# Delta rule of a hybrid decoder: score products in banks of their own, samples' states in two halves from POOL's queue, prompt's state products four steps later

## The chip, the cores and the metric

The kernel runs on one core of one Trainium2 chip, as one program. The metric is the device time of one execution in microseconds (us). Engines are named as in the profile: PE multiplies matrices (PEld loads its stationary operand), DVE, ACT and POOL work on vectors, SP only issues transfers.

## What is computed (the reference, cut)

Two consecutive decoder layers, for a prompt of 256 positions and for 8 samples of 4 positions each (32 rows), which share all weights. Layer 0 mixes tokens by retention, layer 1 by a gated delta rule; each mixer is followed by a gated feed-forward network with a short causal convolution. The change lies in layer 1's mixer alone:

```python
proj = einsum('btd,de->bte', h, w_in)                # q, k, v, gate z, and b, a
conv = silu(causal_dwconv(q|k|v, conv_buf, w_conv))
q, k = l2norm(q) * 128**-0.5, l2norm(k)              # 8 key heads, 16 value heads of 128
beta = sigmoid(b);  g = -exp(a_log) * softplus(a + dt_bias)
def step(S, chunk):                                   # 64 positions of the prompt
    G = cumsum(g);  decay = exp(G_i - G_j), lower triangle
    L = strict_lower((k*beta) @ k.T * decay)          # the scores of the solve
    u, w = solve(I + L, [v*beta, k*beta*exp(G)])
    v_new = u - w @ S
    o = (q*exp(G)) @ S + ((q @ k.T) * decay) @ v_new  # the scores of the attention
    S = S * exp(G_last) + (k*exp(G_last - G)).T @ v_new
out = (rmsnorm(o) * silu(z)) @ w_out
```

For the samples the same rule starts from a stored state S of 128x128 for each of 8 samples and 16 heads, and the 4 new positions form one chunk. The new states of prompt and samples are outputs too.

## The kernel before

**Products.** Every projection is `product` (L525 to L537): the weight tile is split into a rounded part `whi` (ACT, L414) and a rest `wlo` (DVE, L415), the activations likewise, and three passes of 128x288 matmuls are summed; with 1024 inputs that is 24 matmuls to one output tile of 128 columns. The 288 columns are 256 prompt positions and 32 sample rows.

**Order.** Instructions stand on each engine in the order in which a list scheduler puts the program's operations. The program itself is written with generators: after every 6 matmuls of `product` (`QUANTUM`) comes a *tick* (L482), and in each tick all side generators go one `yield` further. `pause(n)` lets n ticks go by, so n times 6 products. A matmul of `product` is called a product below, and positions are told by the number of products counted from the program's start of the mixer's stage.

**The delta-rule stage** works on 4 groups g of 2 key heads and 4 value heads. Its main line is `GDN_ORDER` (L33): K0 V0 K1 A0 Z0 V1 K2 Z1 V2 K3 D0 V3 Z2 D1 D2 Z3 D3, where K are a group's q and k projections, V its values, Z its gate, D its part of the down projection, A a piece of the conditioning vector. K, V, Z and D are 96 products each. Beside it run side generators, for each group: `gdn_decays` (products `pd`, then ACT copies and an exponential into `gat`; POOL's `decay` tiles at L1232 feed them), `gdn_scores`, `gdn_inverse` and levels `pe` (the solve), `gdn_samples` (the samples), `gdn_finish` (the prompt's output and new state).

**Scores** (L1261 to L1284). For each of two key heads j, PE writes `pa` (128x512, L1275) and `pb` (128x256, L1276) from `kqT`; DVE then reads both in eight instructions, L1278 to L1283, into `gnn` (scores of the solve) and `gat` (scores of the attention). DVE's first instruction needs POOL's `ksc` (L1181, L1182), which needs the norms from `pq` (PE L1168) by way of a dozen short DVE instructions. PSUM tiles come from `aux(name, tag)`: tags `a`, `c`, `e` and `s` have one bank of 2 KB per partition each, `b` and `mm` two. Both `pa` have tag `s`, both `pb` tag `a`, each a tile of its own, so j=1 is written when j=0 has been read.

**The samples' states** (L1425 to L1496). A group's states are 2 MB, read as four tiles `gS` of 512 KB (two samples each), from two buffers, by DMAs on SP's queue (L1436). `pks` (L1466) takes 128 matmuls of 128x32 by 128x128, in four runs of 32, one run to a tile; a `gS` tile is loaded again when the run that read its buffer has been issued. The results go through `t` (DVE L1473, ACT L1475) to `psy` (L1480), `t` (DVE L1482), again `psy`, and `pso` (L1489). SP's queue also carries all weights (L400) and the small rearrangements of the solve.

**The prompt's state** (`gdn_finish`). DVE scales the outputs into `on` (L1618, tile name `bigc`); after `pause(STATE_STEPS)`, one tick, PE forms the state `gpS` in 8 matmuls (L1623), whose operands are `kn` and a `bigc` that POOL wrote at L1602.

Of the kernel before, what the change touches and what calls it, by code (L numbers as in the profile page):

```python
# [6 lines left out]
F32 = mybir.dt.float32  # L7
# [7 lines left out]
P = 128  # L15
DM = 1024
KT = DM // P
TP, NB, TD = 256, 8, 4
# [14 lines left out]
GDN_ORDER = [(s[0], int(s[1])) for s in "K0 V0 K1 A0 Z0 V1 K2 Z1 V2 K3 D0 V3 Z2 D1 D2 Z3 D3".split()]  # L33
N_ADA = sum(c == "A" for c, _ in GDN_ORDER)
PAIR_STEPS = (2,2,2,1)
STATE_STEPS = 1
CONV_STEPS = 3
RAW_RET = 3
S_BUFS = 4
# [15 lines left out]
GROUP = 2  # L55
RAW = 4
BIG_C = 4
PA_TAGS = ("sa","sa")
LEVEL_STEPS = 3
LEVEL_TAG = "e"  # L60
GATE_STEPS = 3
SOLVE_STEPS = 1
SAMPLE_STEPS = 3
OUT_STEPS = 1
SQ_ADD = 5
QK_STEPS = 5
# [227 lines left out]
class Program:  # L294
# [660 lines left out]
    def gdn(self, hs, after):  # L955
        nc = self.nc
        with ExitStack() as ctx:
# [17 lines left out]
            nc.gpsimd.memset(self.TA, 0.0)  # L975
            self.gtail = t("gtail", [P, 32, 3])
            self.nexg = None
            self.spawn(self.gdn_gates(hs))
            w = self.weights("wba")
            self.pba = self.mmt("pba")  # L980
# [281 lines left out]
    def gdn_scores(self, g, d):  # L1262

        nc, gp = self.nc, self.gp
        kqT, sc, D = d["kqT"], d["sc"], d["decays"]
        nn = gp.tile([P, 4, 384], F32, tag="gnn", name=f"gnn_{g}", bufs=2)
        at = D[:, 0:12, :].rearrange("p (v b) c -> p v (b c)", b=3)
        for jt, c in ((0, TP - 1), (1, 383)):
            nc.gpsimd.tensor_copy(sc[:, 2, jt, :], at[:, :, c])
        yield  # L1270
        for j in range(2):
            if j:
                yield from self.pause(SCORE_STEPS)
            pa, pa2 = (self.aux(f"p{c}{g}{j}", t) for c, t in zip("ab", PA_TAGS[j]))
            nc.tensor.matmul(pa, lhsT=kqT[:, j, 0, 0:P], rhs=kqT[:, j, :, 0:TP], start=True, stop=True)  # L1275
            nc.tensor.matmul(pa2[:, 0:TP], lhsT=kqT[:, j, 0, P:TP], rhs=kqT[:, j, :, P:TP], start=True, stop=True)  # L1276
            for v in (2 * j, 2 * j + 1):
                nc.vector.scalar_tensor_tensor(nn[:, v, 0:P], pa[:, 0:P], sc[:, 0, 0, v : v + 1], at[:, v, 0:P], ALU.mult, ALU.mult)  # L1278
                nc.vector.scalar_tensor_tensor(nn[:, v, P:TP], pa[:, P:TP], -1.0, at[:, v, P:TP], ALU.mult, ALU.mult)
                nc.vector.scalar_tensor_tensor(nn[:, v, TP:], pa2[:, 0:P], sc[:, 0, 1, v : v + 1], at[:, v, TP:], ALU.mult, ALU.mult)  # L1280
            vs = slice(2 * j, 2 * j + 2)
            nc.vector.tensor_tensor(at[:, vs, 0:TP], pa[:, TP:].unsqueeze(1).to_broadcast([P, 2, TP]), at[:, vs, 0:TP], ALU.mult)
            nc.vector.tensor_tensor(at[:, vs, TP:], pa2[:, P:TP].unsqueeze(1).to_broadcast([P, 2, P]), at[:, vs, TP:], ALU.mult)  # L1283
        d.update(at=at, nn=nn)  # L1284
# [133 lines left out]
    def gdn_gate(self, g, hs, d):  # L1418
# [3 lines left out]
            self.nc.scalar.activation(sz[:, m, :], p, AF.Silu)  # L1422
        d["sz"] = sz

    def gdn_samples(self, g, a):  # L1425

        nc, gp, A = self.nc, self.gp, self.A
# [1 line left out]
        big = lambda sh, dt=F32: self.big(sh, dt, "s", 512, 3, 1)  # L1429
        small = lambda: gp.tile([P, P], F32, tag="t05", name=f"t05_{g}", bufs=8)  # L1430
        kqd, rr, vs = a["kqd"], a["rr"], a["vs"]
        S = []

        def load(u):
            S.append(t("gS", [P, 2, 4, P], bufs=2))
            nc.sync.dma_start(S[-1], A["sg"][g][:, 2 * u : 2 * u + 2])  # L1436

        load(0)
        load(1)

        sc = t("ssc", [P, 3], bufs=1)
        nc.vector.tensor_scalar(sc[:, 0:1], self.bs[:, g : g + 1], rr[:, 8:9], rr[:, 8:9], ALU.mult, ALU.mult)
# [14 lines left out]
        nc.vector.scalar_tensor_tensor(db, pas[:, 0:P], sc[:, 1:2], db, ALU.mult, ALU.mult)  # L1457
        nc.vector.tensor_tensor(du, pas[:, P : 2 * P], du, ALU.mult)
        pks = self.aux(f"pks{g}", "c")
        for bb in range(NB):  # L1460
            if bb % 2 == 0:
                yield

            for s in range(2):
                for v in range(4):
                    nc.tensor.matmul(  # L1466
                        pks[32 * v : 32 * v + 32, s * P : (s + 1) * P], lhsT=kqm[s][:, v // 2, bb, :], rhs=S[bb // 2][:, bb % 2, v, :],
                        start=(bb == 0 and s == 0), stop=(bb == NB - 1 and s == 1), skip_group_check=True,
                    )
            if bb % 2 and bb < 4:  # L1470
                load(bb // 2 + 2)
        r = small()
        nc.vector.scalar_tensor_tensor(r, pks[:, 0:P], self.nexg[:, g : g + 1], vs, ALU.mult, ALU.add)  # L1473
        qg = small()
# [255 lines left out]
```

## Time and profile before

| what | us |
|---|---|
| median of 3 runs | 1231.98 |
| the three runs | 1230.52 to 1234.35 |
| the profiled execution, its own time | 1235.09 |
| span of its trace, first to last instruction | 1233.3 |
| PE busy in the span | 1162.4 (94%) |
| DVE busy | 877.2 (71%) |
| ACT, POOL busy | 608.4 (49%), 326.0 (26%) |
| stage of the delta rule | about 592 to 990 |

PE is the busiest engine, so a stretch in which PE is not busy is where time is lost. DVE is next, and within the delta-rule stage its share is higher than over the whole span. The clock in the table by stretches is the granted clock of PE as a share of full speed.

### The profile page before, as it was taken

How to read it: one execution, taken by the hardware profiler on the slowest of the kernel's cores; microseconds unless marked ns; L12 is line 12 of the kernel's file. 1: busy time of each engine (PE TensorE's matmuls, PEld its weight loads, DVE VectorE, ACT ScalarE, POOL GpSimd, SP SyncE). 2: the span in 40 equal slices, each digit the busy share in tenths (PEclk: the TensorE clock that was granted, in tenths of full speed). 3: DMA queues.
4: the chain of work that ended last, by engine and by line, in shares of the span. 5: the costliest groups of instructions: out<-in, count | busy, mean ns of one | idle time of the engine just before them, and what ended most of it. 6: DMA issues, size and time to landing. Idle time of an engine off the chain costs nothing.

```text
span 1233.3 us, 24974 instructions
## 1 busy us (share of the span) xinstructions
PE 1162.4 (94%) x9486; PEld 1045.2 (85%) x9486; DVE 877.2 (71%) x2038; ACT 608.4 (49%) x1258; POOL 326.0 (26%) x504
## 2 busy tenths in 40 slices
PE   6999999999999999999889888988899899999996
PEld 2879788797969999997777777977789699999996
DVE  3657574765766666667769888797965687878785
ACT  2444534344446445543674655745544365555542
POOL 0214142151301221233242124243222212233241
PEclk9999999999999999999989998999999899999997
DMA  9999696866689556556636652534334997878521
GB/s 350 347 335 331 224 338 230 315 239 236 226 298 400 196 161 199 171 181 243 219 84 209 218 165 61 161 129 120 126 109 130 307 358 257 258 238 264 182 76 39
DMA packets 97480, 269.08 MB, mean 218 GB/s; under 512 B 26816, under 2 KB 28832, under 8 KB 97232
## 3 DMA queue, kind: packets, MB, share of 16 engines
q1 hardware_dynamic: 87456, 234.42, 56.6%
q0 software_dynamic: 8032, 29.16, 6.3%
q10 hardware_dynamic: 1872, 3.90, 0.9%
q8 instruction: 75, 1.23, 0.4%
q14 instruction: 45, 0.37, 0.1%
HBM read 236.06 MB, written 31.39 MB: 217 GB/s over the span
## 4 chain that ended last, share of the span: by engine, by line
PE 77%; DVE 13%; ACT 3%; DMA 3%; issue 2%; POOL 1%; ACTq 0%; POOLq 0%; DVEq 0%
PE down L533 17%; PE fg L533 12%; PE fv L533 11%; PE pg L533 4%; PE pv L533 4%; PE adaP L453 4%; PE p L533 3%; PE gv L533 2%; PE gz L533 2%; DVE mp L1319 2%; DVE wlo L415 2%; PE gk L533 2%; PE pO L884 1%; PE pU L903 1%; PE pS L854 1%
## 5 line engine op out<-in xcount | busy, mean ns | idle before, releaser
L415 DVE TENSOR_TENSOR wlo<-more,whi 128x1024 fp32r<-128x1024 f32 x138 | 171.1, 1241 | 80.6 <-ACT whi L414 67.8
L414 ACT CAST whi<-more 128x1024 fp32r<-128x1024 f32 x138 | 144.4, 1048 | 139.6 <-PE down L533 53.3
L414 ACT CAST whi<-raw 128x1024 fp32r<-128x1024 f32 x123 | 128.0, 1044 | 146.3 <-PE down L533 44.1
L415 DVE TENSOR_TENSOR wlo<-raw,whi 128x1024 fp32r<-128x1024 f32 x123 | 154.2, 1256 | 60.6 <-ACT whi L414 36.5
L702 POOL TENSOR_TENSOR x<-x,dt 128x32 f32<-128x32 f32 x159 | 103.1, 649 | 138.9 <-DVE dt L700 137.2
L698 DVE SCALAR_TENSOR_TENSOR x<-down,mod,x 128x256 f32<-128x256 f32 x160 | 76.7, 479 | 52.5 <-PE down L533 51.9
L580 POOL TENSOR_TENSOR fal<-cv,fah 128x288 fp32r<-128x288 f32 x44 | 41.2, 936 | 217.3 <-ACT fah L579 186.3
L533 PE MATMUL down<-fal,whi 128*128 128x288 f32 x352 | 64.5, 295 | 0.0
L533 PE MATMUL down<-fah,whi 128*128 128x288 f32 x352 | 62.2, 294 | 0.0
L533 PE MATMUL down<-fah,wlo 128*128 128x288 f32 x352 | 62.1, 294 | 0.0
L904 DVE SCALAR_TENSOR_TENSOR S<-S,pU 128x512 f32<-128x512 f32 x64 | 42.2, 684 | 24.5 <-PE pU L903 24.4
L533 PE MATMUL fg<-hh_ffn,whi 128*128 128x288 f32 x352 | 58.4, 298 | 0.8 <-ACT hh_ffn L626 0.7
L533 PE MATMUL fv<-hh_ffn,whi 128*128 128x288 f32 x352 | 58.7, 297 | 0.0
L533 PE MATMUL fg<-hh_ffn,wlo 128*128 128x288 f32 x352 | 55.0, 296 | 0.0
L533 PE MATMUL fv<-hh_ffn,wlo 128*128 128x288 f32 x352 | 54.7, 295 | 0.0
L533 PE MATMUL fv<-hl_ffn,whi 128*128 128x288 f32 x352 | 54.2, 295 | 0.0
L533 PEld LDWEIGHTS fg<-hh_ffn,whi 128*128 128x128 f32 x352 | 50.3, 188 | 4.6 <-ACT hh_ffn L632 2.2
L533 PE MATMUL fg<-hl_ffn,whi 128*128 128x288 f32 x352 | 54.0, 295 | 0.0
L533 PEld LDWEIGHTS down<-fal,whi 128*128 128x128 f32 x352 | 52.4, 188 | 0.4 <-issue 0.4
L533 PEld LDWEIGHTS down<-fah,whi 128*128 128x128 f32 x352 | 51.9, 188 | 0.8 <-ACT whi L414 0.8
L533 PEld LDWEIGHTS fv<-hh_ffn,whi 128*128 128x128 f32 x352 | 50.3, 188 | 2.5 <-ACT ftail L934 1.2
L533 PEld LDWEIGHTS down<-fah,wlo 128*128 128x128 f32 x352 | 51.9, 188 | 0.0
(467 smaller groups left out, 2921.3 us busy)
## 6 DMA issues: line engine op xcount, KB each, us to landing
more<-in_wu SPq DMA_DIRECT2D x73, 512.0 KB, 5.2
raw<-in_wada SPq DMA_DIRECT2D x69, 512.0 KB, 4.8
raw<-in_wgi SPq DMA_DIRECT2D x48, 512.0 KB, 3.9
more<-in_wada SPq DMA_DIRECT2D x43, 512.0 KB, 6.3
more<-in_wd SPq DMA_DIRECT2D x36, 512.0 KB, 3.8
S<-in_sr SPq DMA_DIRECT2D x16, 1024.0 KB, 8.5
out_rs<-S POOLq DMA_DIRECT2D x16, 1024.0 KB, 6.9
raw<-in_wri SPq DMA_DIRECT2D x28, 512.0 KB, 4.6
```

Source lines behind the costliest of these rows:

```text
L414: nc.scalar.copy(hi[:, :c], r)
L415: nc.vector.tensor_tensor(lo[:, :c], r, hi[:, :c].bitcast(F32), ALU.subtract)
L453: nc.tensor.matmul(self.adaP[32 * g : 32 * g + 32, 0:256], lhsT=self.cs[:, k, :], rhs=rv[:, :, g, :], start=(k == 0), stop=(k == KT - 1), ...
L533: self.nc.tensor.matmul(out, lhsT=av[:, k, c0 : c0 + m], rhs=b[:, k, :], start=(k0 == 0 and i == 0), stop=(k1 == kts and i == len(seq) - 1))
L580: (nc.gpsimd if pool_lo else nc.vector).tensor_tensor(lo, src, hi.bitcast(F32), ALU.subtract)
L698: nc.vector.scalar_tensor_tensor(xm[:, :TP], p[:, :TP], g[:, 0:1], xm[:, :TP], ALU.mult, ALU.add)
L702: (nc.vector if gate == 11 and last and m == KT - 1 else nc.gpsimd).tensor_tensor(xv, xv, t, ALU.add)
L854: nc.tensor.matmul(pS, lhsT=kt[:, j, c * P : (c + 1) * P], rhs=vt[:, j, :], start=(j == 0), stop=(j == 1))
L884: nc.tensor.matmul(pO4[32 * g : 32 * g + 32, :], lhsT=qm[:, c, 4 * bb + g, :], rhs=S[bb, c][:, g, :], start=(bb == 0 and c == 0), stop=Fal ...
L903: nc.tensor.matmul(pU, lhsT=kms[g][:, c * P : (c + 1) * P], rhs=vst, start=True, stop=True)
L904: nc.vector.scalar_tensor_tensor(S[bb, c][:, g, :], S[bb, c][:, g, :], gamma4, pU, ALU.mult, ALU.add)
L1319: nc.vector.tensor_tensor(m, Ti[:, 0:k, :].rearrange("p j c -> p c j").unsqueeze(1).to_broadcast([P, w, 8, k]), X[:, 0:k, i:k].rearrange(" ...
```

## The change

Four things, all in the delta-rule stage:

1. **Scores.** `PA_TAGS` becomes "se": `pa` of j=0 stays in bank `s`, `pa` of j=1 goes to bank `e`, which `pd` and `pe` use as well. The two `pb` become halves of one tile `pb` in bank `a`, side by side in columns; it is taken once per group.
2. **States in halves.** `gdn_samples` no longer reads four runs of 32 `pks` matmuls with a load behind each, but two runs of 64 with 9 ticks between (`HALF_STEPS`). A new `half_states` loads two tiles at once. The second half's loads are issued behind the first run, and the next group's first half behind the second run, so a group finds its first half on the way (`self.states`).
3. **Queue.** These 16 loads move from SP's to POOL's queue. There are still two buffers.
4. **`STATE_STEPS`** goes from 1 to 4: `gpS` comes 3 ticks later.

The counts of matmuls and of bytes don't change.

```diff
-STATE_STEPS = 1
+STATE_STEPS = 4
-PA_TAGS = ("sa","sa")
+PA_TAGS = "se"
+HALF_STEPS = 9
...
         for j in range(2):
             if j:
                 yield from self.pause(SCORE_STEPS)
-            pa, pa2 = (self.aux(f"p{c}{g}{j}", t) for c, t in zip("ab", PA_TAGS[j]))
+            pa = self.aux(f"pa{g}{j}", PA_TAGS[j])
+            if j == 0:
+                both = self.aux(f"pb{g}", "a")
+            pa2 = both[:, j * TP : (j + 1) * TP]
             nc.tensor.matmul(pa, lhsT=kqT[:, j, 0, 0:P], rhs=kqT[:, j, :, 0:TP], start=True, stop=True)
-            nc.tensor.matmul(pa2[:, 0:TP], lhsT=kqT[:, j, 0, P:TP], rhs=kqT[:, j, :, P:TP], start=True, stop=True)
+            nc.tensor.matmul(pa2, lhsT=kqT[:, j, 0, P:TP], rhs=kqT[:, j, :, P:TP], start=True, stop=True)
...
+    def half_states(self, g, half):
+        S = []
+        for u in (2 * half, 2 * half + 1):
+            S.append(self.gp.tile([P, 2, 4, P], F32, tag="gS", name=f"gS_{g}{u}", bufs=2))
+            self.nc.gpsimd.dma_start(S[-1], self.A["sg"][g][:, 2 * u : 2 * u + 2])
+        return S
...
-            nc.sync.dma_start(S[-1], A["sg"][g][:, 2 * u : 2 * u + 2])
-
-        load(0)
-        load(1)
+        S = self.states or self.half_states(g, 0)
...
-        for bb in range(NB):
-            if bb % 2 == 0:
-                yield
...
-            if bb % 2 and bb < 4:
-                load(bb // 2 + 2)
+        for half in range(2):
+            yield from self.pause(HALF_STEPS if half else 1)
+
+            for bb in range(4 * half, 4 * half + 4):
...
+            if half == 0:
+                S = self.half_states(g, 1)
+            else:
+                self.states = self.half_states(g + 1, 0) if g < 3 else None
```

**How instructions move: PE where V0 ends and K1 begins.** `gv` are products of V0, `gk` of K1, `pd` the next group's decay products (three rounds, one bank `e`), `pv` transposes of values. Before:

```order
L533 MATMUL gv_7376<-hh_gdn,whi 128x288 x7
L533 MATMUL gv_7376<-hl_gdn,whi 128x288 x3
L1275 MATMUL pa_7303<-kqT_6862 128x512
L1276 MATMUL pb_7304<-kqT_6862 128x256
L533 MATMUL gv_7376<-hl_gdn,whi 128x288
L1246 MATMUL pd_7389<-decay_7323,after_r 128x256 x2
L1247 MATMUL pd_7389<-never,ident_r 128x256
L1249 MATMUL pd_7389<-decay_7323,ones_r 128x128 x2
L533 MATMUL gv_7376<-hl_gdn,whi 128x288 x4
L533 MATMUL gv_7376<-hh_gdn,wlo 128x288 x8
L1246 MATMUL pd_7448<-decay_7397,after_r 128x256 x2
```

After, from the last products of V0 on:

```order
L534 MATMUL gv_7437<-hl_gdn,whi 128x288 x8
L534 MATMUL gv_7437<-hh_gdn,wlo 128x288 x8
L1281 MATMUL pb_7280<-kqT_6862 128x256
L1248 MATMUL pd_7314<-decay_7252,after_r 128x256 x2
L1249 MATMUL pd_7314<-never,ident_r 128x256
L1251 MATMUL pd_7314<-decay_7252,ones_r 128x128 x2
L1412 MATMUL pv_7324<-cst,gcv 128x128 x2
L1248 MATMUL pd_7388<-decay_7322,after_r 128x256 x2
L1249 MATMUL pd_7388<-never,ident_r 128x256
L1251 MATMUL pd_7388<-decay_7322,ones_r 128x128 x2
L1412 MATMUL pv_7408<-cst,gcv 128x128 x2
L1248 MATMUL pd_7447<-decay_7396,after_r 128x256 x2
```

The second `pb` (j=1) has moved 37 products later, behind the whole of V0, and its `pa` has moved ahead of it, out of this excerpt; `pd` of three rounds, which had products between them, now stand in a row behind that `pb` and ahead of K1's first product.

**POOL at the same place.** `gnn` MEMSETs clear blocks of the scores once ACT has copied them out; `decay` feeds the next `pd`. Before:

```order
L1182 TENSOR_SCALAR ksc_7227<-ksc_7227 128x8
L1269 COPY ksc_7227<-gat_6987 128x4 x2
L1455 TENSOR_TENSOR t_0_7608<-gat_6987,cst_g 128x128
L1456 TENSOR_TENSOR t_0_7609<-gat_6987,cst_g 128x128
L1232 TENSOR_TENSOR decay_7323<-cst_g,ghl 128x512
L1232 TENSOR_TENSOR decay_7397<-cst_g,ghl 128x512
L1299 MEMSET gnn_7241 32x4x2x32 x4
L1232 TENSOR_TENSOR decay_8664<-cst_g,ghl 128x512
```

After:

```order
L1184 TENSOR_SCALAR ksc_7227<-ksc_7227 128x8
L1394 COPY gvsT_7163<-gcv 128x32
L1304 MEMSET gnn_7241 32x4x2x32 x4
L1234 TENSOR_TENSOR decay_7322<-cst_g,ghl 128x512
L1234 TENSOR_TENSOR decay_7396<-cst_g,ghl 128x512
L1234 TENSOR_TENSOR decay_8662<-cst_g,ghl 128x512
```

The four MEMSETs now stand ahead of three `decay`, where two of these `decay` stood ahead of the MEMSETs.

**PE at the end of K2.** `pks` of group 1 and the state `gpS` of group 0; `gk` are K2's products, `gz` those of Z1. Before, the last three runs of `pks`, and further on `gpS`:

```order
L1466 MATMUL pks_8554<-gS_8518,bigs 32x128 x16
L533 MATMUL gk_8621<-hh_gdn,whi 128x288 x2
L533 MATMUL gk_8621<-hl_gdn,whi 128x288 x4
L1466 MATMUL pks_8554<-gS_8601,bigs 32x128 x16
L533 MATMUL gk_8621<-hl_gdn,whi 128x288 x4
L533 MATMUL gk_8621<-hh_gdn,wlo 128x288 x8
L1466 MATMUL pks_8554<-gS_8661,bigs 32x128 x16
```

and

```order
L533 MATMUL gk_8806<-hh_gdn,wlo 128x288 x2
L1246 MATMUL pd_8832<-decay_8784,after_r 128x256 x2
L1247 MATMUL pd_8832<-never,ident_r 128x256
L1249 MATMUL pd_8832<-decay_8784,ones_r 128x128 x2
L1623 MATMUL gpS_8757<-bigc,kn_6863 128x256 x4
```

After, the second half of `pks` and `gpS`:

```order
L534 MATMUL gk_8758<-hh_gdn,wlo 128x288 x2
L1248 MATMUL pd_8790<-decay_8736,after_r 128x256 x2
L1249 MATMUL pd_8790<-never,ident_r 128x256
L1251 MATMUL pd_8790<-decay_8736,ones_r 128x128 x2
L534 MATMUL gk_8758<-hh_gdn,wlo 128x288 x6
L1471 MATMUL pks_8552<-gS_8615,bigs 32x128 x16
L1471 MATMUL pks_8552<-gS_8617,bigs 32x128 x16
L1248 MATMUL pd_8871<-decay_8798,after_r 128x256 x2
L1249 MATMUL pd_8871<-never,ident_r 128x256
L1251 MATMUL pd_8871<-decay_8798,ones_r 128x128
L1631 MATMUL gpS_8774<-bigc,kn_6863 128x256 x4
```

The second half's tiles are read in one piece, 48 products behind the first half, where before two products-runs of 6 and 12 lay between the last three reads; `gpS` stands behind it. At the following groups `gpS` (position 1782 before, 1772 after; 2073 before, 2064 after) stands ahead of the second half of `pks` (1806 and 2094). On SP the 16 loads no longer stand between the weights; on POOL they stand in pairs, the first pair of the program directly behind the MEMSET of `TA` (L976), the pair of group 0's second half with the three short instructions of the solve's `X` (L1314 to L1317) around its second load.

**PE at the end of D0.** `down` are D0's products, `pe` a level of group 2's solve, `pb_10080` and `pb_10049` the second `pb` of group 3. Before:

```order
L533 MATMUL down<-gah_8890,wlo 128x288 x4
L1275 MATMUL pa_10079<-kqT_9443 128x512
L1276 MATMUL pb_10080<-kqT_9443 128x256
L533 MATMUL down<-gah_8890,whi 128x288 x4
L533 MATMUL down<-gal_8891,whi 128x288 x4
L533 MATMUL down<-gah_8890,wlo 128x288 x4
L1345 MATMUL pe_10147<-uc_10104,gnn_9015 32x32 x16
```

After:

```order
L534 MATMUL down<-gah_8932,wlo 128x288 x4
L534 MATMUL down<-gah_8932,whi 128x288 x4
L534 MATMUL down<-gal_8933,whi 128x288 x4
L534 MATMUL down<-gah_8932,wlo 128x288 x4
L1281 MATMUL pb_10049<-kqT_9457 128x256
L1350 MATMUL pe_10098<-uc_10039,gnn_8972 32x32 x16
L1457 MATMUL pas_10725<-kqd_9459 128x256
```

The `pb` stands 24 products later than before, and the `pe`, which takes bank `e`, directly behind it; before, 12 products lay between the two.

## Rows read from the trace of the kernel before


**Rows 1.** The page's busy times, with shares of the span and instructions.

```profile
PE 1162.4 (94%) x9486; PEld 1045.2 (85%) x9486; DVE 877.2 (71%) x2038; ACT 608.4 (49%) x1258; POOL 326.0 (26%) x504
```

**Rows 2.** Busy time by stretches of the delta-rule stage; columns: the stretch, its length, busy us of each engine with its instructions, the granted clock as a share of full speed, the DMA engines' share and GB/s. 643 to 665 is K1, 665 to 692 Z0, 707 to 744 K2, 790 to 823 K3, 823 to 852 D0, 869 to 902 Z2 with the start of D1; the last row is the sum over 592 to 990.

```profile
643.00:665.00 22.00, 19.54 (x238) 17.30 (x236) 16.97 (x53) 14.78 (x41) 5.18 (x13) 1.00 0.77 232
...
665.00:692.00 27.00, 23.68 (x189) 18.61 (x190) 24.62 (x67) 10.55 (x23) 5.70 (x11) 1.00 0.62 206
...
707.00:744.00 37.00, 33.02 (x394) 29.37 (x393) 30.71 (x89) 22.12 (x76) 12.40 (x27) 1.00 0.50 145
...
790.00:823.00 33.00, 29.51 (x318) 27.02 (x317) 30.18 (x86) 17.98 (x68) 11.02 (x22) 1.00 0.51 157
...
823.00:852.00 29.00, 24.05 (x214) 19.74 (x213) 26.34 (x79) 13.98 (x31) 13.75 (x26) 0.94 0.30 83
...
869.00:902.00 33.00, 28.34 (x281) 24.59 (x280) 29.89 (x73) 12.07 (x40) 7.34 (x12) 0.90 0.34 110
...
sum 398.00, PE 357.40 PEld 315.96 DVE 316.96 ACT 218.60 POOL 116.72; mean PE 22.34 PEld 19.75 DVE 19.81 ACT 13.66 POOL 7.30
```

**Rows 3.** What PE waited for between 580 and 985 us; columns: who waited, for what, us in total, times, longest.

```profile
PE pa L1275 <- DVE gat L1282: 6.9, 3, 2.9
...
PE pks L1466 <- DMA gS<-in_sg: 5.9, 6, 2.0
...
PE gpS L1623 <- DVE bigc L1618: 4.5, 3, 2.5
...
PE psy L1480 <- DVE t L1482: 2.3, 2, 2.2
...
PE psy L1480 <- ACT t L1475: 1.9, 2, 1.7
```

**Rows 4.** PE's timeline at the places where it waited for `gS`, for `bigc` and for the `t` of `psy`; columns: start, us, engine and line, the operation, how many in a row, and in brackets the idle time before with what ended it.

```profile
656.72 1.08 PE L1466 MATMUL pks<-gS,bigs 128*32 128x128 f32 x32 [0.43 <-DMA gS<-in_sg]
...
731.28 1.08 PE L1466 MATMUL pks<-gS,bigs 128*32 128x128 f32 x32 [0.90 <-DMA gS<-in_sg]
...
736.43 0.49 PE L1480 MATMUL psy<-t,t 128*128 128x128 f32 x2 [1.70 <-ACT t L1475]
...
739.33 1.99 PE L1623 MATMUL gpS<-bigc,kn 128*128 128x256 f32 x8 [1.09 <-DVE bigc L1618]
...
808.54 1.08 PE L1466 MATMUL pks<-gS,bigs 128*32 128x128 f32 x32 [0.79 <-DMA gS<-in_sg]
...
813.51 1.08 PE L1466 MATMUL pks<-gS,bigs 128*32 128x128 f32 x32 [1.70 <-DMA gS<-in_sg]
...
816.52 1.99 PE L1623 MATMUL gpS<-bigc,kn 128*128 128x256 f32 x8 [0.93 <-DVE bigc L1618]
...
891.14 0.41 PE L1466 MATMUL pks<-gS,bigs 128*32 128x128 f32 x2 [1.97 <-DMA gS<-in_sg]
...
894.05 3.75 PE L1623 MATMUL gpS<-bigc,kn 128*128 128x256 f32 x8 [2.51 <-DVE bigc L1618]
...
897.73 1.93 PE L1466 MATMUL pks<-gS,bigs 128*32 128x128 f32 x30
```

**Rows 5.** By tile, the loads `gS` on SP's queue: ns of an issue (least, median, most), first and last start, and us to landing.

```profile
L1436 SPq DMA_DIRECT2D gS<-in_sg x16: 327/328/537, 595.7 to 886.6; - x16
...
DMA to landing us min/median/max: 3.8/4.6/6.3
```

**Rows 6.** By tile, the stores `out_gs` of the new states, 512 KB each like the loads, on POOL's queue later in the program; columns as in the group above.

```profile
L1546 POOL DMA_DIRECT2D out_gs<-uS x16: 555/572/574, 1011.3 to 1199.2; - x16
...
DMA to landing us min/median/max: 2.9/4.0/6.1
```

**Rows 7.** What SP's queue waited for between 580 and 985 us; columns as for PE's waits.

```profile
SPq L1436 <- PE pks L1466: 21.9, 8, 7.4
```

**Rows 8.** The chain of waits in 580 to 985 us; a stretch of products that nothing held up; columns: start, us, what.

```profile
942.84 12.82 PE gz L533 x96
```

**Rows 9.** PE's timeline around group 0's scores and the start of K1; columns as above.

```profile
620.49 0.50 PE L1168 MATMUL pq<-ones,t1m 128*128 128x1 f32 x4
...
631.01 2.08 PE L1275 MATMUL pa<-kqT 128*128 128x512 f32 x2 [2.90 <-DVE gat L1282]
...
642.78 1.41 PE L533 MATMUL gk<-hh_gdn,whi 128*128 128x288 f32 x8
```

**Rows 10.** DVE's timeline at the same place: first and last instruction of j=0, and the first of j=1.

```profile
628.84 0.35 DVE L1278 SCALAR_TENSOR_TENSOR gnn<-pa,ksc,gat 128x128 f32<-128x128 f32 x1 [2.74 <-POOL ksc L1182]
...
630.87 0.41 DVE L1283 TENSOR_TENSOR gat<-pb,gat 128x256 f32<-128x256 f32 x1
...
633.12 0.35 DVE L1278 SCALAR_TENSOR_TENSOR gnn<-pa,ksc,gat 128x128 f32<-128x128 f32 x1 [0.90 <-PE pa L1275]
```

**Rows 11.** POOL's timeline at the same place: the last MEMSET of `gnn` and the `decay` behind it.

```profile
639.57 0.31 POOL L1299 MEMSET gnn<- 32x256 f32 x1 [0.76 <-PE pd L1251]
639.96 1.05 POOL L1232 TENSOR_TENSOR decay<-cst_g,ghl 128x512 fp32r<-128x512 f32 x1
```

**Rows 12.** PE's timeline at the end of D0: the `pa` of j=1 of group 3, and the level `pe` of group 2.

```profile
842.00 2.07 PE L1275 MATMUL pa<-kqT 128*128 128x512 f32 x2 [2.17 <-DVE gat L1282]
...
847.36 0.69 PE L1345 MATMUL pe<-uc,gnn 32*32 32x32 f32 x32 [0.60 <-DVE uc L1334]
```

More of the change, by code (lines that the diff above doesn't have):

```diff
@@ L977, in gdn @@
             self.nexg = None
+            self.states = None
             self.spawn(self.gdn_gates(hs))
@@ L1431, in gdn_samples @@
         kqd, rr, vs = a["kqd"], a["rr"], a["vs"]
-        S = []
-        def load(u):
-            S.append(t("gS", [P, 2, 4, P], bufs=2))
-            nc.sync.dma_start(S[-1], A["sg"][g][:, 2 * u : 2 * u + 2])
-        load(0)
-        load(1)
+        S = self.states or self.half_states(g, 0)
         sc = t("ssc", [P, 3], bufs=1)
@@ L1459, in gdn_samples @@
         pks = self.aux(f"pks{g}", "c")
-        for bb in range(NB):
-            if bb % 2 == 0:
-                yield
[L1464 to L1469, printed above, removed]
-            if bb % 2 and bb < 4:
-                load(bb // 2 + 2)
+        for half in range(2):
+            yield from self.pause(HALF_STEPS if half else 1)
+            for bb in range(4 * half, 4 * half + 4):
+                for s in range(2):
+                    for v in range(4):
+                        nc.tensor.matmul(
+                            pks[32 * v : 32 * v + 32, s * P : (s + 1) * P], lhsT=kqm[s][:, v // 2, bb, :], rhs=S[bb // 2 % 2][:, bb % 2, v, :],
+                            start=(bb == 0 and s == 0), stop=(bb == NB - 1 and s == 1), skip_group_check=True,
+                        )
+            if half == 0:
+                S = self.half_states(g, 1)
+            else:
+                self.states = self.half_states(g + 1, 0) if g < 3 else None
         r = small()
```

## The prediction

> **What bounds the kernel now.** I read the busy times first. PE is busy for 1162.4 of 1233.3 us [rows 1], so the kernel ends when PE has got through its work, and an edit that leaves PE's work alone can only win or lose idle time of PE. The change touches the delta-rule stage. There the table by stretches comes next [rows 2]: of 398 us PE is busy for 357.4, so about 40 us are lost. DVE is close behind in four stretches: 24.62 of 27 us in Z0, 30.18 of 33 in K3, 26.34 of 29 in D0, 29.89 of 33 in Z2. What DVE leaves idle there (2.4, 2.8, 2.7 and 3.1 us) is a ceiling on what PE can win in the stretch, because PE's products are consumed by DVE. K1 and K2 have room: DVE leaves 5.0 of 22 and 6.3 of 37 us.
>
> Then the list of what PE waited for [rows 3]: 6.9 us for the scores' bank, 5.9 for the samples' states, 4.5 for `bigc` ahead of `gpS`, 2.3 and 1.9 in `psy`. The change aims at the first three. PE's timeline shows where they lie [rows 4]. It also shows that a wait can cost more than itself: `gpS` took 3.75 us at 894.05 and 1.99 at 816.52 for the same 8 matmuls, after 1.97 and 2.51 us of idle PE; the granted clock in that stretch is 0.90 [rows 2], a mean of stretches at 2.4 GHz and at 1.2 GHz.
>
> The sum is made against the profiled execution's own 1235.1 us and then carried to the median of 1232.0, which is 3.1 us lower.
>
> **The states in halves, on POOL's queue.** PE's work is the same 512 matmuls and no bytes are added. Before, a load was issued behind the run that read its buffer, one or two runs ahead of its use; SP's queue stood 21.9 us behind those runs [rows 7]. After, 48 products lie between the first half and the second. At the pace of undisturbed products, 12.82/96 = 0.134 us [rows 8], that is 6.4 us at least, against 4.6 us median and 6.3 us longest from issue to landing [rows 5]. The next group's first half has far more. So the waits for `gS` go: 0.43 in K1, 0.90 in K2, 0.79 and 1.70 in K3, 1.97 in Z2 [rows 4].
>
> What does POOL's queue cost? The trace has no such load there, but 16 stores of the same size: 572 ns to issue and 4.0 us to land [rows 6], against 328 ns and 4.6 us on SP [rows 5]. I take the stores' price. 16 x 0.57 = 9 us of POOL are spread over some 300 us of an engine that is 26% busy [rows 1]. What is queued behind a waiting load on POOL are `kqd`, `bigs`, `ksc`, `decay` and `qs`, needed later than the load by their places in the order, so I cost it at nothing. Without that cover a `decay` would come late by one wait of PE, up to 2.0 us as with the loads now [rows 3]. Weights on SP gain from an emptier queue, but PE hardly waited for them: nothing.
>
> **The prompt's states later.** Three ticks are 18 products or 2.4 us; the longest wait for `bigc` is 2.51 us [rows 4]. So this wait goes where `bigc` is not itself delayed: 1.09 in K2, 0.93 in K3, 2.51 in Z2. Its consumers are the stores of the state and `px`, which waits for the gate: nothing.
>
> **What of these gains PE keeps.** K1 0.4 and K2 0.90 + 1.09 = 2.0, in full, since DVE has room. K2's wait of 1.70 in `psy` stays: in the changed order 10 products lie between the last `pks` and that `psy`, 12 before. In Z0 the long `psy` wait (2.2 [rows 3]) is for DVE's `t` and its place moves little; I take half, 1.0. In K3 the waits sum to 3.4 and DVE's room is 2.8; part of that room is DVE waiting for other things, so I take 2.0. In Z2 it is 1.97 + 2.51 = 4.5, and about 2.7 more for the lower clock (3.75 - 1.99 for `gpS`; 1.93 against 1.08 for 30 and 32 `pks`), 7.2 together, with 3.1 of room on DVE; I take 3.0. The sum is **-8.4 us**.
>
> **The score products.** This is the part where the words of the change and its order differ. In the old form the second `pa` waited for DVE's reads of the first, 2.90 us at group 0 and 2.17 at group 3 [rows 9, 12], 6.9 in all at three groups [rows 3]. With a bank of its own `pa` of j=1 no longer waits. But the second `pb` is now in the tile of the first and carries a wait for DVE, and it comes right after. Its place on PE is later by 37 products at group 0 and 24 at group 3, earlier by 10 and 42 at groups 1 and 2. DVE cannot start on j=0 before `ksc`, and j=0 then takes 628.84 to 631.28, 2.4 us [rows 10], so the wait moves and does not vanish. The extremes are 6.9 us won and 6.9 lost (every wait gone, or twice as long); the row nearest to the new wait is the old wait on the same DVE instructions, so I take **0**.
>
> The Trainium skill (PSUM — Partial Sum Buffer, section "PSUM bank collisions raise a hardware error") speaks against this edit: PSUM is to be guarded by bank and quadrant, not by address. By it the two halves of `pb`, though in different columns, must not be written and read at once. The changed order agrees, with a wait for DVE ahead of the second `pb`; no row of the trace shows two users of one bank at different addresses. Where the page's rule decides everything, the second rival below comes out.
>
> **The start of K1.** Here the order adds something. Three rounds of `pd` and the second `pb` now stand in a row ahead of K1, in one bank, and two of the three `decay` are behind four MEMSETs of `gnn` on POOL, which wait for the scores' copies by ACT. The last MEMSET of before began at 639.57 and the `decay` behind it ran 639.96 to 641.01 [rows 11]. Two more `decay` at 1.05 us after it bring the last round to 642.1 at the earliest, and its six matmuls, at 0.134 us each, to 642.9, where K1 began at 642.78 in before [rows 9]. Group 0's last `pq` comes 19 products later as well, 2.5 us, and with it all scores and MEMSETs. Between 0 and two waits as long as the longest score wait (2 x 2.9 = 5.8), I take **+2.0**, nearer to the `decay` rows.
>
> **Group 2's solve at the end of D0.** `pe` stands directly behind the second `pb` of group 3, in the bank of the second `pa`, so it waits for DVE's reads of that `pa`, up to 2.4 us. In exchange PE arrives there 24 products (3.2 us) later, by when j=0 has been read and the 2.17 us wait [rows 12] is gone. I take 0.
>
> **Sum.** -8.4 + 0 + 2.0 + 0 = -6.4 us: 1228.7 for an execution like the profiled one, **about 1226** on the median of 1232.0.
>
> **The rivals.**
> *First: all waits go.* `pb` is covered as well, and DVE does not hold PE back. Then 6.9 + 5.9 + 4.5 + 4.2 = 21.5 us of rows 3 and 2.7 for the clock in Z2 could go, 24 in all; with a third of it given back to DVE's ceiling, 16 remain: **1216**. For it speaks that K1 and K2 have room on DVE; against it that four stretches leave DVE 3.1 us or less.
> *Second: the waits only change places.* The second `pb` waits at all four groups, where three waited before, and in Z0, K3, D0 and Z2 DVE sets the pace. Then only K1 and K2 keep their 2.4 us, less the 2.0 at K1's start: **1231.6**, no change. DVE's 316.96 us busy in the 398 [rows 2] speak for it in part only: a fifth of the stage is free on DVE. That the scores do not do what the words say belongs here.
> *Third: slower by the row of `pd` ahead of K1.* If the late `pq`, the wait at `pb` and the MEMSETs add up one behind another, PE stands still through most of 633 to 645. Price: the 5.8 us above, the lower clock behind it, which cost 1.8 us in the row of `gpS` (3.75 against 1.99) and would come at K1 and once more, 3.6, and 2 us of new waiting at group 1, where less cover is left: +11.4, less the 2.4 kept in K1 and K2, +9 on the 1232.0, about **1240**. It decides from the point where the last `decay` ends later than about 645. For it speaks the order on POOL; against it that PE had slack there before as well, with waits of its own.
>
> **How the numbers follow.** My forecast (1221 to 1229) has 0.45, the first rival 0.12, the second 0.23, the third 0.20. A measurement of this kernel tells about 0.3% from no change, 1228.3 to 1235.7. Faster takes the first rival and most of the forecast's range: 0.53. Same takes the rest and the second rival: 0.27. Slower: 0.20. The range from 1214 to 1240 reaches into the rivals at both ends; both signs of the unknown price of the scores (6.9 about 1226 is 1219 to 1233) lie in it. The likeliest case alone is 1221 to 1229.
>
> **What would show it.** In the profile of the changed kernel: no row of `pks` waiting for `gS`; no wait of `gpS` over 1 us; a granted clock near 1.00 in Z2; a wait at the second `pb` of 1 to 4 us in at least two groups; the first product of K1 within 2 us of its old distance from the stage's start. I am wrong if the second `pb` does not wait, if POOL's loads land later than the 6.4 us of cover, or if PE's idle time shrinks and the stretches do not, which would make DVE the bound of the whole stage.

## The result

The changed kernel takes 1245.6 us (median of 4 runs, 1244.5 to 1249.0) against 1233.2 us before in the same comparison: a ratio of 1.0108, with a 95% interval of 1.0084 to 1.0132. By that ratio it is slower by some 13 us. The forecast was 1226, faster. One execution of all that follow (of e3 below, 1595.2 us at a granted clock of 0.66, where the others have 0.97 to 0.99) fell into a slower state and is in no ratio.

The profiled execution's span is 1244.3 us, 11.0 longer than before. PE's busy time is the same within 1.4 us, so 9.6 us of the difference are time in which PE stood. The lower clock lengthens the busy time itself, as in K0 below (19.6 us busy against 16.6):

```profile
PE 1163.8 (94%) x9486; PEld 1049.4 (84%) x9486; DVE 878.2 (71%) x2038; ACT 609.3 (49%) x1258; POOL 339.0 (27%) x520
```

The table by stretches of the changed kernel, one row each for K0, V0, K1, Z0, K2, K3, D0 and Z2, from where its products begin to where those of the next stretch do, and the sum over K0 to the end of D2 (columns as in [rows 2]). K0's row begins among the last products `pba`, those of b and a, at the same place of the order in both kernels; K0's own first 8 products ran before it:

```profile
596.53:622.91 26.38, 19.58 (x125) 18.41 (x122) 15.80 (x54) 15.35 (x40) 7.20 (x12) 0.87 0.55 180
...
622.91:655.41 32.50, 25.31 (x159) 22.05 (x157) 21.05 (x63) 21.23 (x51) 16.12 (x31) 0.87 0.34 97
...
655.41:674.31 18.90, 17.85 (x173) 16.50 (x173) 13.05 (x39) 13.88 (x39) 6.80 (x16) 0.96 0.45 131
...
674.31:704.55 30.24, 26.38 (x250) 20.15 (x251) 27.75 (x79) 8.95 (x16) 6.58 (x13) 1.00 0.64 210
...
720.97:759.98 39.01, 32.45 (x340) 29.61 (x339) 32.70 (x87) 20.28 (x69) 16.93 (x30) 0.91 0.45 131
...
801.02:833.10 32.08, 27.45 (x248) 26.06 (x247) 29.67 (x81) 17.28 (x66) 16.07 (x24) 0.95 0.40 114
...
833.10:866.17 33.07, 26.91 (x289) 23.01 (x287) 28.20 (x84) 17.46 (x34) 14.34 (x29) 0.90 0.37 109
...
882.94:909.51 26.57, 22.75 (x206) 21.22 (x205) 26.08 (x68) 10.78 (x35) 7.44 (x13) 0.94 0.41 131
...
sum 356.77, PE 313.86 PEld 284.03 DVE 286.99 ACT 199.10 POOL 120.93; mean PE 22.42 PEld 20.29 DVE 20.50 ACT 14.22 POOL 8.64
```

The same for the kernel before, K0, V0, and the whole from K0 to the end of D2:

```profile
592.79:612.07 19.28, 16.56 (x119) 15.26 (x117) 15.43 (x52) 14.68 (x37) 4.76 (x8) 1.00 0.72 239
...
612.07:642.78 30.71, 25.74 (x162) 23.11 (x162) 23.43 (x64) 20.76 (x51) 17.04 (x32) 0.89 0.19 49
...
592.79:942.68 349.89, 314.33 (x2895) 280.46 (x2893) 287.25 (x779) 198.23 (x524) 107.61 (x206) 0.96 0.46 140
```

K0 is 7.1 us longer than before, at a granted clock of 0.87 where it was 1.00, and V0 1.8 us longer. Over the whole of K0 to D2 it is 356.8 against 349.9 us, 6.9 more: from V0 on, what one stretch loses (Z0, K2, D0, D1 with D2) another returns (K1, V2, Z2, which was 32.85 us). Of the 11 us, 3.7 lie ahead of the stage, where all engines run the same order as before; in the experiments' executions the stage begins between 583.6 and 584.9 us, here at 586.7 and before at 582.9, so those 3.7 us differ from one execution to the next and don't belong to the change.

What PE waited for (580 to 1000 us, columns as in [rows 3]):

```profile
PE gpS L1631 <- DVE bigc L1626: 13.3, 3, 5.4
...
PE gk L534 <- DVE sp L1049: 6.4, 1, 6.4
...
PE pb L1281 <- DVE gat L1288: 4.7, 3, 2.3
...
PE pd L1248 <- POOL decay L1234: 3.2, 4, 1.7
...
PE pd L1248 <- DVE gat L1287: 1.6, 1, 1.6
...
PE pe L1350 <- DVE gat L1287: 1.5, 1, 1.5
```

The waits for `gS` are gone, all of them. In their place stand 13.3 us for `bigc` (4.5 before), a single wait of 6.4 us for `sp` in K0, 4.7 for the second `pb`, and waits of `pd` and `pe`.

**K0.** `sp` is the first of a chain of short DVE instructions on the decay rates, and needs `dtb`, 8 KB that ACT's queue loads. The timelines of POOL, DVE and PE, and by tile the landing of `dtb` in the changed kernel:

```profile
596.53 1.11 POOL L1434 DMA_DIRECT2D gS<-in_sg  x2
...
606.78 0.21 DVE L1035 TENSOR_TENSOR sp<-bt,dtb 128x48 f32<-128x48 f32 x1 [2.68 <-DMA dtb<-in_dtb]
...
610.40 2.26 PE L534 MATMUL gk<-hh_gdn,whi 128*128 128x288 f32 x8 [6.37 <-DVE sp L1049]
...
DMA to landing us min/median/max: 8.7/8.7/8.7
```

and before, the issue and landing of `dtb` and SP's issues of the first two `gS`:

```profile
L1030 ACTq DMA_DIRECT2D dtb<-in_dtb x1: 450/450/450, 594.3 to 594.3; - x1
...
DMA to landing us min/median/max: 4.1/4.1/4.1
...
595.68 0.33 SPq L1436 DMA_DIRECT2D gS<-in_sg  x1
...
599.80 0.43 SPq L1436 DMA_DIRECT2D gS<-in_sg  x1
```

The two loads of 512 KB start at 596.5 on POOL's queue. ACT issues `dtb` at 598.0, and it lands 8.7 us later instead of 4.1. Before, the first `gS` load stood on SP's queue in one row with the weights, and was issued 1.4 us behind `dtb` where it is now 1.5 us ahead of it; the second was issued when `dtb` had landed. So the move changed two things at once, the queue and the place in time.

`dtb` was not the only load that came late. `alog`, issued just ahead of it, took 7.0 us (4.3 before), and a weight tile that SP issued at 599.0 took 7.7 us and landed with `dtb` at 606.7, where the one issued at 595.2 before took 4.3. The edit also puts ACT's `bt`, the other operand of `sp`, behind a cast `whi`, but `bt` was written 5.7 us before `dtb` landed.

**V0 into K1.** PE and POOL, in the changed kernel:

```profile
645.62 0.70 PE L1281 MATMUL pb<-kqT 128*128 128x256 f32 x2 [2.30 <-DVE gat L1288]
...
647.91 0.77 PE L1248 MATMUL pd<-decay,after_r 128*128 128x256 f32 x2 [1.59 <-DVE gat L1287]
...
651.32 0.80 PE L1248 MATMUL pd<-decay,after_r 128*128 128x256 f32 x2 [1.66 <-POOL decay L1234]
...
647.66 0.30 POOL L1304 MEMSET gnn<- 32x256 f32 x1 [4.43 <-ACT t1k L1301]
...
649.36 1.90 POOL L1234 TENSOR_TENSOR decay<-cst_g,ghl 128x512 fp32r<-128x512 f32 x1
```

PE waits for DVE at the second `pb`, again for DVE at the first `pd` (bank `e` still holds the second `pa`), and then for a `decay` that stands behind the MEMSETs and took 1.90 us where most take 1.05 (the last section shows why).

### The profile page after: what moved, and what is told of

Its sections match the earlier page's. It is cut to its first block, busy times and chain, and to the rows that moved or that the text cites. A ratio compares the mean times of both kernels' runs of the same rounds, so it can differ in the third digit from the quotient of the medians.

```text
span 1244.3 us, 24968 instructions
## 1 busy us (share of the span) xinstructions
PE 1163.8 (94%) x9486; PEld 1049.4 (84%) x9486; DVE 878.2 (71%) x2038; ACT 609.3 (49%) x1258; POOL 339.0 (27%) x520
## 4 chain that ended last, share of the span: by engine, by line
PE 76%; DVE 13%; DMA 5%; ACT 3%; issue 2%; POOL 2%; SPq 0%; POOLq 0%; DVEq 0%; ACTq 0%
PE down L534 17%; PE fg L534 11%; PE fv L534 11%; PE pv L534 4%; PE pg L534 4%; PE adaP L454 4%; PE p L534 3%; PE gv L534 3%; PE gz L534 2%; DVE mp L1324 2%; DVE wlo L416 2%; PE gk L534 1%; PE pU L904 1%; PE pO L885 1%; DVE Ti L1328 1%
## 5 line engine op out<-in xcount | busy, mean ns | idle before, releaser
L454 PE MATMUL adaP<-raw,c 128*32 128x256 f32 x552 | 48.8, 401 | 4.5 <-DMA raw<-in_wada 4.5
```

Of the source, the lines that this page charges most:

```text
L454: nc.tensor.matmul(self.adaP[32 * g : 32 * g + 32, 0:256], lhsT=self.cs[:, k, :], rhs=rv[:, :, g, :], start=(k == 0), stop=(k == KT - 1), ...
```

## The experiments

Ratios are to the kernel before, run in the same comparison, with 95% intervals. Each kernel tried has a short name, e1 to k8, given with its result. How far one trace may be trusted was measured on the way: the kernel of f1 below turned out to have the order of before on all five engines, row for row; its stretch K0 to D2 took 343.1 us in its trace, where the trace of before has 349.9. So a difference of a few us between two traces is not by itself an effect of an edit; verdicts on the time rest on the medians.

### The first pair of loads

```diff
-            self.nc.gpsimd.dma_start(S[-1], ...)
+            eng = self.nc.sync if g == 0 and half == 0 else self.nc.gpsimd
+            eng.dma_start(S[-1], ...)
```

> The changed kernel, but group 0's first two loads go back to SP's queue; the other 14 stay on POOL's. Theory A (the first pair, alone on POOL's queue and 1 MB large, starts ahead of the small loads of alog and dtb on ACT's queue and delays them; K0 took 26.4 us in the changed kernel against 19.3): dtb lands in 4 to 5 us again (8.7 in the changed kernel, 4.1 before), PE's wait for sp goes from 6.4 to under 2.5 us, K0 takes 19 to 20 us, and the time falls by 6 to 8 us to 1237 to 1240. Theory B (the loss lies in the scores and in waits that changed places later in the stage): K0 may be shorter, but DVE gives it back, and the time stays at 1244 to 1247.

Measured (e1): 1240.0 us, ratio 1.0052 (1.0032 to 1.0073), so the 1.08% shrink by half. `dtb` lands in 3.0 us, K0 takes 18.8 us, and the wait for `sp` is 1.2 us.

```profile
DMA to landing us min/median/max: 3.0/3.0/3.0
```

All 16 loads on SP (`self.nc.sync.dma_start` in `half_states`):

> The changed kernel with all 16 loads on SP's queue, still in halves. Theory A: as with the first pair on SP, 1237 to 1240, since the other 14 loads are covered on either queue; at most 2 us between this and that kernel. Rival: POOL's queue costs something at every load (POOL waited 19.3 us for pks there), then this is another 3 us or more faster, 1234 or less. Rival: SP blocks the weights behind loads that wait, then slower than with only the first pair on SP by 2 us or more.

Measured (e2): 1239.2 us, ratio 1.0045 (1.0027 to 1.0063), the same as with the first pair alone. A difference between the two queues for the other 14 loads is not seen; one of up to some 3 us would not stand out from these intervals.

From the other side, the kernel before with only its first two loads moved:

```diff
-            nc.sync.dma_start(S[-1], ...)
+            (nc.gpsimd if g == 0 and u < 2 else nc.sync).dma_start(S[-1], ...)
```

> The kernel before with one edit: group 0's first two loads on POOL's queue. Theory A: dtb lands after 8 to 9 us, K0 takes 25 to 27 us, and the time is 6 to 8 us above before, 1239 to 1241. Theory B: within 2 us of before, 1231 to 1235.

Measured (e3): 1240.3 us (median of three, 1239.7 to 1244.4), ratio 1.0067 (1.0043 to 1.0092), some 8 us slower by this one edit. By tile `dtb`, and by PE's waits:

```profile
DMA to landing us min/median/max: 8.3/8.3/8.3
...
PE gk L533 <- DVE sp L1047: 6.0, 1, 6.0
```

K0 took 26.0 us. Theory A held both ways: the first pair's move is what costs. Whether it costs by the queue or by being issued ahead of `dtb` is not told apart, since no kernel has the pair on POOL's queue behind `dtb`.

### The scores

The scores' part alone on the kernel before (the diff of the change at L1273, and `PA_TAGS = "se"`):

> The kernel before with the scores' part alone (pa of j=1 in bank e, both pb in one tile of bank a). Theory A: the wait only moves from the second pa to the second pb, within 2 us of before, 1231 to 1235. Theory B (the scores' part, with pd in a row ahead of K1 and pe behind pb, is what loses): 1238 or more, V0 longer than 33 us (30.7 before, 32.5 in the changed kernel) and D0 longer than 32 us (29.0 before, 33.1 in the changed kernel).

Measured (e4): 1241.9 us, ratio 1.0069 (1.0053 to 1.0084). Theory B was right here in the time and in V0, theory A (the wait only moves) wrong. V0 took 35.3 us and D0 31.7, just under the 32 that theory B wanted. PE's, POOL's and DVE's timelines at the end of V0:

```profile
640.07 0.80 PE L1246 MATMUL pd<-decay,after_r 128*128 128x256 f32 x2 [3.99 <-POOL decay L1232]
...
635.75 1.09 POOL L1302 MEMSET gnn<- 32x256 f32 x3 [0.19 <-ACT t1k L1299]
...
636.92 3.09 POOL L1232 TENSOR_TENSOR decay<-cst_g,ghl 128x512 fp32r<-128x512 f32 x1
...
636.75 2.36 DVE L415 TENSOR_TENSOR wlo<-raw,whi 128x1024 fp32r<-128x1024 f32 x2
```

PE stands 3.99 us at a `pd` for a `decay` that starts only behind the MEMSETs, and these wait for the scores. Of the 3.99 us, 2.0 are not the order on POOL: the `decay` took 3.09 us instead of 1.05, beside two `wlo` of DVE. The wait at the second `pb` was 0.66 us at this place. Two further kernels separate bank `e` from the joint `pb`. First the joint `pb` alone (`PA_TAGS = "ss"`):

> The kernel before with both pb in one tile of bank a, and both pa still in bank s. Theory A (what costs in the scores' part is bank e: pd and pe must wait for DVE's reads of the second pa, and are lined up behind it): within 1.5 us of before, V0 30 to 31 us. Theory B (the wait of the second pb for DVE's reads of the first half is the cost): 1238 or more, V0 34 us or more.

Measured (f1): 1232.0 us, ratio 0.9988 (0.9971 to 1.0006): no difference, and the order on all engines is that of before. V0 took 28.3 us in its trace, against 30.7 in that of before, so two traces of one order differ by 2.4 us here. Then bank `e` alone, with `pb` tiles of their own:

```diff
-PA_TAGS = ("sa","sa")
+PA_TAGS = ("sa","ea")
```

> The kernel before with the second pa in bank e, and the two pb in tiles of their own, one after the other in bank a. Theory A (bank e): 1239 to 1243, as with the whole scores' part, V0 about 35 us. Theory B (the joint pb): within 2 us of before.

Measured (f2): 1243.5 us, ratio 1.0079 (1.0060 to 1.0097), with V0 at 34.3 us. Its order on all engines is that of e4, so the joint `pb` changes no order with either bank. It is bank `e`. And the scores' part with the second `pa` in bank `c` (`PA_TAGS = "sc"`):

> The kernel before with both pb in one tile and the second pa in bank c, which holds pas and pks and at this place neither pd nor pe. Theory A (bank e is what costs): pd stands where it stood before, V0 29 to 31 us, D0 28 to 30 us, and the time is within 2 us of before, 1231 to 1235. Rival (any place other than bank s moves the wait to a worse one): 1238 or more.

Measured (f3): 1230.8 us, ratio 0.9977 (0.9958 to 0.9996), V0 28.6 us, D0 29.4. POOL's timeline at the same place as above, and PE's waits at the second `pb` in f2 and in f3:

```profile
635.50 1.05 POOL L1232 TENSOR_TENSOR decay<-cst_g,ghl 128x512 fp32r<-128x512 f32 x1 [2.46 <-PE pd L1249]
...
636.49 1.38 POOL L1302 MEMSET gnn<- 32x256 f32 x4
...
PE pb L1276 <- DVE gat L1283: 8.7, 3, 3.4
...
PE pb L1279 <- DVE gat L1286: 4.3, 3, 2.5
```

The `decay` is ahead of the MEMSETs again. The second `pb` waits with two tiles (f2) as with one (f3), and the kernel that waits 4.3 us there is not slower than before. This is the fastest kernel tried; but f1, which has the order of before, measured 0.9988, so a gain over before is not shown beyond doubt.

### Four steps

The kernel before with `STATE_STEPS = 4` alone:

> The kernel before with STATE_STEPS 4 alone. The prediction's step: gpS stands 2.4 us later, the waits for bigc (4.5 us in three) shrink below 1.5 us and the time falls by 1 to 3 us. Rival (bigc is late because DVE is; the changed kernel waits 13.3 us for it in spite of the later place): the waits stay at 3 us or more and the time stays within 1 us of before.

Measured (e6): 1233.3 us, ratio 0.9997 (0.9981 to 1.0013). By PE's waits, and `gpS` of group 1 on PE:

```profile
PE gpS L1623 <- DVE bigc L1618: 4.0, 3, 2.2
...
814.12 2.00 PE L1623 MATMUL gpS<-bigc,kn 128*128 128x256 f32 x8 [1.28 <-DVE bigc L1618]
...
816.17 1.08 PE L1466 MATMUL pks<-gS,bigs 128*32 128x128 f32 x32
```

4.5 us before, 4.0 here, three waits in both. That is what the rival expected, but the run does not show its reason, for the longer pause did not put `gpS` later. Here this `gpS` stands ahead of the last run of `pks`, where in before it stood behind it (813.51 and 816.52 in [rows 4]). Counted in the traces, `gpS` is at the same product as before for group 0, and 13 and 11 products earlier for groups 1 and 2. A later `gpS` alone is tested in no run, and why a longer pause led the scheduler to an earlier place is open.

### The halves

The changed kernel with the old scores and the first pair on SP:

> The changed kernel without the scores' part and with group 0's first two loads on SP's queue: states in halves, 14 loads on POOL's queue and STATE_STEPS 4 remain. If the losses are the first pair and the scores, and the two other parts win what was forecast for them, this is below before: 1225 to 1230. If what they win is given back to DVE: 1231 to 1235.

Measured (e8): 1239.2 us, ratio 1.0047 (1.0032 to 1.0062). Neither forecast held: the halves, at 9 steps, with 14 loads on POOL's queue and four steps, lose 6 us without the scores and the first pair. The trace shows 10.6 us of waits for `bigc`, and in Z0 a new thing. The order of PE there has 16 products `adaP` (of the conditioning vector, with weights from the same buffers as all others) at product 1248, where before they began at 1225. SP's queue (640 to 692 us, before and in that kernel) and PE in that kernel:

```profile
SPq L400 <- PE adaP L453: 14.5, 4, 5.4
...
SPq L401 <- PE adaP L454: 21.7, 3, 16.1
...
681.56 2.29 PE L534 MATMUL gz<-hh_gdn,whi 128*128 128x288 f32 x8 [2.13 <-ACT whi L415]
...
692.50 1.22 PE L534 MATMUL gz<-hh_gdn,wlo 128*128 128x288 f32 x8
```

SP stands 16.1 us at a weight buffer that `adaP` still holds (5.4 at the longest before); then `gz` waits for its weights, and the 8 products behind the wait take 2.29 us where 8 further on take 1.22. The granted clock is 0.52 from 681.5 to 687.5 us, the lower level of 1.2 GHz, and 1.00 from 692.5 on. A distance of 8 steps brings an order in which `adaP` stands earlier:

```diff
-HALF_STEPS = 9
+HALF_STEPS = 8
```

> The kernel of e8_old_scores with HALF_STEPS 8 in place of 9, nothing else. In its order the products adaP of the conditioning vector stand in Z0 at products 1235, 1248, 1272, 1296 (before: 1225, 1248, 1272, 1296), where with 9 steps 16 of them stand together at 1248. Theory C (the halves lose because adaP comes late in Z0, so its weights keep their buffers, SP's queue stands 16 us, and gz waits for its weights at the lower clock): SP's wait for adaP in 640 to 692 us falls below 10 us, Z0 takes 27 to 29 us (31.8 with 9 steps), and the time falls by 3 us or more, to 1233 to 1236. Theory D (the halves lose elsewhere, by gpS waiting for bigc 10.6 us and by the solve): within 2 us of e8_old_scores.

Measured (g1): 1234.1 us, ratio 1.0017 (0.9994 to 1.0041), Z0 28.6 us where it was 31.8. The time fell as theory C has it (the two intervals meet only at their ends), though SP's wait for `adaP` is 16.8 us in all, with a longest of 11.2, and not below 10:

```profile
SPq L401 <- PE adaP L454: 16.8, 4, 11.2
```

> As above with HALF_STEPS 3: the second half's loads have 18 products or 2.4 us ahead of their use, less than they take to land. Theory C: adaP at 1234, so Z0 is short as with 8 steps, but pks waits for gS again, 2 us or more in each of four groups, and the time is 1234 to 1240. If the distance of the halves doesn't matter since DVE sets the pace, it is within 2 us of the one with 8 steps.

Measured (g2): 1233.9 us, ratio 1.0012 (0.9991 to 1.0034). PE waits for `gS` again, though less than expected, and no cost is seen against the one with 8 steps, which has no such wait; a cost of up to some 3 us would not stand out:

```profile
PE pks L1469 <- DMA gS<-in_sg: 3.5, 4, 1.9
```

### All parts, with the three faults taken out

```diff
-PA_TAGS = "se"
+PA_TAGS = "sc"
-HALF_STEPS = 9
+HALF_STEPS = 8
...
+            eng = self.nc.sync if g == 0 and half == 0 else self.nc.gpsimd
```

> The changed kernel with three edits: the second pa in bank c in place of e, HALF_STEPS 8, and group 0's first two loads on SP's queue. All four parts of the change are in it. If bank e, the adaP order and the first pair are the whole of the loss, and the halves win nothing: 1229 to 1234 (as f3_pa_in_c, 1230.8). If the parts also win what the prediction summed for them once the three are gone (8.4 us): 1222 to 1228. If a loss is left that the three do not explain: 1236 or more.

Measured (k8): 1233.7 us, ratio 0.9992 (0.9975 to 1.0009). The whole loss is gone, and no gain is left. Its larger waits of PE:

```profile
PE pb L1281 <- DVE gat L1288: 4.2, 3, 2.1
...
PE pd L1248 <- ACT gat L1256: 3.3, 1, 3.3
...
PE gpS L1632 <- DVE bigc L1627: 2.9, 2, 1.6
```

## Why the prediction was wrong

Of the signs that the prediction named, two came: no `pks` waited for `gS`, and the second `pb` waited (three times, 2.3 us at the longest). Three did not: `gpS` waited up to 5.4 us, the granted clock in Z2 was 0.94, and K1's first product came 58.9 us after the start of K0's row, where it had been 50.0.

**The loads on POOL's queue, costed at nothing.** This step failed first, and in the changed kernel it is over half of the loss. I asked what a load costs POOL, what it blocks on POOL, and whether it lands in time. For 14 of the 16 the runs give no other answer: e2 and e1 are equal, and `pks` never waits for `gS` in the changed kernel. For the first two I did not ask who else loads at that moment. On SP's queue, in one row with the weights, they were issued behind `dtb`; on a queue of their own they were issued ahead of it and ran beside that row, and a load of 8 KB on a third queue landed 4.6 us later. Price: 7 to 8 us (1.0108 against 1.0052, and 1.0067 on before). The Trainium skill (DMA: Bandwidth & Descriptors, section "SWDGE vs HWDGE vs iDMA") says that within each DMA engine hardware and software queues are internal queues of their own, served in turn. The later landings of `dtb`, `alog` and SP's weights beside the two loads agree with it; they do not show how much is the queue and how much the earlier issue.

**The scores, taken at 0.** The bounds were 6.9 us either way; f2 and e4, which have one order, lose 10 and 8 us. The row of `pd` behind the scores and the MEMSETs ahead of `decay` were seen and priced at +2.0 for the start of K1, and as the third rival at up to 5.8 with the clock behind it (the rival's +9 on 1232.0 make 1241, not 1240). The rival had the mechanism, the forecast the wrong end of its range: V0 took 35.3 us in e4 and 34.3 in f2, against 30.7 in the trace of before and 28.3 in f1, which has the same order as before. D0, also taken at 0, took 31.7 in e4, against 29.0 and 27.0, and K3, for which the scores had no term, 37.2 against 32.9 and 34.3. The nearest row was not the old wait for `gat`, but the chain score, ACT's copy, MEMSET, `decay`, `pd`, which the order put on PE's path. One link was priced too low: `decay` at 1.05 us took 3.09 in e4, beside DVE's `wlo`.

**The joint `pb`.** The second rival rested on it. A wait at the second `pb` is there (4.7 us in three), as the text said, but the joint tile is not its reason: f2 has two tiles and waits 8.7 us there, in the order of e4. Both `pb` shared the one bank `a` before too, and there the wait at the second `pa` (6.9 us before, 6.8 in f1) came just ahead of it. By itself the wait costs nothing that f3 shows. The rule that I quoted from the Trainium skill (PSUM — Partial Sum Buffer, section "PSUM bank collisions raise a hardware error") is obeyed by the order, in both forms.

**The halves and the later state, -8.4 us.** The waits for `gS` vanished as said, and the time did not follow. In g2 3.5 us of these waits are back and the time is that of g1: they seem to have lain beside DVE's work, also in K2, where I had counted them in full, though a cost of up to some 3 us would not stand out there. For `gpS` the step that failed is "three ticks are 18 products or 2.4 us": the pause was counted, not the order. By the order of the change itself `gpS` stands 10 and 9 products earlier at groups 1 and 2 (1772 against 1782, 2064 against 2073), and, counted in the traces, only 6 later at group 0. PE then waited 13.3 us for it, where the prediction had no wait over 1 us. At group 0, PE stood ready 29.1 us after K2's first product (31.2 before), and DVE's `bigc` let it start after 34.5 (32.2). Place alone does not decide: in e8 and k8 `gpS` of group 2 stands 9 products later than in before, and waits 4.1 us in the one and not at all in the other. What a `gpS` that is later in every group could win is open; k8, with all four parts, wins none of it. That DVE's idle time is not time that PE can have is the reading that fits, and was not tested alone.

**What the order did elsewhere.** With 9 steps the halves moved `adaP` in Z0. The prediction costed the places that the diff names, not that one. That e8 loses 6 us is measured, and that g1 loses less; g1 by itself is not told from before. That `adaP` is the cause is likely from SP's 16.1 us and the `gz` behind it, but not isolated, since another distance moves other rows too and SP's total wait hardly fell.

**The parts don't add.** Alone, first pair, scores and halves cost 8, 8 and 6 us; together 13. With halves and scores both present (e1) the loss is 6, no more than with the halves alone (e8). Against e8, V0 is longer by 4.3 us in e1, and K3, D0 and Z2 are shorter by 0.8 to 2.4. One overlap of first pair and scores can be seen: V0 takes 35.0 us in e1, where a `pd` waits 4.0 us for a `decay` beside two `wlo`, and 32.5 in the changed kernel, where the `decay` meets the rest of one `wlo` and the wait is 1.7. Why the stretches behind return the rest I could not settle.

## What to carry to other kernels

A load that moves to an idle queue is no longer in line with the others and may start ahead of them: list what else is loading in those microseconds, the smallest loads first, and who waits for them. A wait on PE is worth its time only if the engine that feeds PE would have been ready; take the wait away in a kernel of its own before counting on it. And where a scheduler sets the order, compare the whole order of the busy engine, not the places that the diff names: a bank shared with a producer of later work, or one step more in a pause, moved rows far from the edit, and a longer pause moved its own rows earlier.

## What was unexpected

An 8 KB load took 8.7 us to land (8.3 in e3) behind two loads of 512 KB that had just been issued on another queue, and 2.9 to 5.1 us in the twelve executions without them. The loads on POOL's queue landed in 5.0 us (median; the longest, 9.3, is of the first pair) against 4.6 (longest 6.3) on SP, at 556 ns an issue against 328:

```profile
L1434 POOL DMA_DIRECT2D gS<-in_sg x16: 528/556/592, 596.5 to 896.1; - x16
...
DMA to landing us min/median/max: 4.1/5.0/9.3
```

A `decay` on POOL, 1.05 us in most rows, took 3.09 us in e4 and 1.90 us in the changed kernel at the same place. The traces tell what it ran against: DVE's `wlo`, a TENSOR_TENSOR of 1.22 us. In e4 the `decay` began at 636.92, inside two `wlo` that ran to 639.1, and ended 0.9 us behind them. Of the 224 `decay` in the 14 traces, 29 took over 1.5 us, and each of these had a `wlo`, or one of DVE's TENSOR_TENSOR `mp` and `gal`, running at its start or starting within 0.1 us. Where the `decay` came first, the `wlo` took longer instead: in before, beside a `decay` that ran from 612.20 for 1.05 us,

```profile
612.33 2.00 DVE L415 TENSOR_TENSOR wlo<-raw,whi 128x1024 fp32r<-128x1024 f32 x1 [0.21 <-issue]
```

So these instructions of POOL and DVE took turns, and a chain through POOL has to be priced with what DVE does beside it.
